# One more pair of gates taken plainly, a store moved to another queue, and operands split earlier at three stage ends

## The chip, the cores and the metric

The kernel runs on one core of one Trainium2 chip. The metric is the device time of one execution in microseconds (us). PE is the matrix engine (TensorE), DVE the vector engine, ACT the scalar engine, POOL is GpSimd, and SP is the queue from which most transfers are issued. POOL has a queue of its own for transfers.

## The reference

One transformer-like layer on a sequence of 1024 tokens of width 1024, in fp32. What matters here, cut down:

```python
h = rmsnorm(x, g_mix_pre) * (1.0 + scale_m) + shift_m
z = h @ w_in                      # q, k, v, forget, pool, conv columns, and 3 x 1024 gate columns gl
br_a = forgetting_attention(q, k, v, fl + b_f)       # 8 heads x 64
br_b = pool_mixer(pu, w_pool, pool_scale)            # 256 columns
br_c = short_conv(ch, cb, cc, conv_w)                # 256 columns
gates = sigmoid(gl).reshape(b, s, 3, d)
merged = gates[0]*(br_a @ wa) + gates[1]*(br_b @ wb) + gates[2]*(br_c @ wc)
x  = x + gate_m * rmsnorm(merged @ w_out, g_mix_post)
h2 = rmsnorm(x, g_ff_pre) * (1.0 + scale_f) + shift_f
return x + gate_f * rmsnorm(square(relu(h2 @ w_ff1)) @ w_ff2, g_ff_post)
```

## The kernel before, in words

Every fp32 operand of a matrix product is split into two parts that PE takes at full rate: a high part (ACT copies it, names ending in h or hi) and a low part (DVE subtracts the high part, names ending in l or lo). A product is then three matmuls: high by high, high by low, low by high. `split` (lines 113 to 115) and `fsplit` (686 to 688) are these two instructions. Nearly every matmul is 128x128 by 128x512.

The stages, one after the other on PE: normalisation and the v columns; the attention with its projections; the gates; the branches; the output projection with the second normalisation and the transposes of `h2` (`out_tile`, `h2T_pair`); the first feed-forward matrix (FFN1); the second (FFN2); the final norm. The order of the instructions on each engine is set when the program is built, by a scheduler that works from the order of the code and the dependences; each engine then runs its own list in that order, and each instruction waits for what it needs. So an instruction that waits also holds up what stands behind it on its engine or queue.

**Gates.** There are 24 blocks of 128 gate columns: 3 branches b by 8 column blocks j. `gate(j, b)` (line 607) takes one block plainly: `load_w`, then two halves of 24 matmuls each in a "mm" bank (`gemm_T`, line 343), each half followed by a sigmoid on ACT (line 610) and a store to DRAM on POOL's queue. Two blocks, (0, 1) and (1, 1), are taken so (lines 731, 732); their matmuls stand among those of the attention. The other 22 are taken two at a time by `gate_pair` (line 796), a Strassen-like scheme with 7 products of 12 matmuls, 84 instead of 96. It needs sums of halves of `h` (t1p, t2p, g, sn: lines 751 to 782) and of the weights: `o` is the split of the first weight block r1, `o21` that of a sum s21 with the second block r2 (`sums_21`), `o34` and `o4` come from `sums_34`. The loop over `todo` (line 857) runs 11 pairs; each pair from the second on also loads four tiles of w_ada, which DVE reduces (`more_ada`). `mod_rows` (line 665), behind the pair i == 9, transposes two small rows of gate vectors on PE and stores them to `gr_d` on the SP queue (line 677). The M pool has 8 slots of 4 KB a partition, taken in turn by weights, sums, branch operands and the two `gr` rows.

**Branches.** `to_branches` (line 850), called inside the last pair, splits the branch operands 4 to 7 (loaded by `load_br` ahead of the last pair); behind the loop the operands 0 to 3 are loaded, then three gates (`load_sig`), then the first block of w_branch (`load_wb`, line 908). The loop over j (line 920) takes 48 matmuls a step.

**FFN1.** Bank names are X, Y and Z. `first_two(j)` (line 1085) computes the first two products of pair j and `relu2` (DVE, line 1073) squares the rectified sum; five of these (`EARLY`) run ahead while ACT and DVE build the sums T1 to T4. `last_five(j)` does the rest; its last lines rectify bank X on ACT (1110) and square on DVE. `h2T_pair(3, ...)` transposes the last quarter of `h2` in between, in the two Z banks.

**FFN2.** `parts` (line 1194) splits one step's operands u and w on ACT and DVE, `step` (1184) issues its 24 matmuls.

## Time and profile before

| | |
|---|---|
| time, median of 3 runs (lowest, highest) | 1501.37 us (1499.16, 1501.98) |
| the profiled execution: its time, its span | 1502.08 us, 1500.2 us |
| mean granted clock of PE | 0.976 of 2.4 GHz |
| busy share: PE, DVE, ACT, POOL | 95%, 68%, 42%, 15% |
| data moved over the span | 209 MB, 139 GB/s |

All times in the views are us from the start of the span. The span is 1.9 us shorter than the execution's time. PE is busy for 1422.0 us of 1500.2: nearly all of the rest lies in the stage ends, and the views that show where are the waits of PE (summed by the line that waited and by what released it) and the timeline (each row: start, duration, engine, line, operation, written<-read tiles, shape, and in brackets the idle time ahead of it with what ended that). A matmul's duration is longer than its share of the pipeline; what one costs is the step from one start to the next.

### The profile page before, as it was taken

What the parts mean: (1) busy time and instruction counts of PE and PEld (TensorE: products, weight loads), DVE (VectorE), ACT (ScalarE), POOL (GpSimd) and SP (SyncE); (2) the same over time, 40 slices, a digit from 0 to 9 for tenths busy, and PEclk for the clock granted to TensorE, in tenths of its full rate; (3) what the DMA queues carried; (4) which work ended last, traced back from release to release, by engine and by line L of the source; (5) the groups of instructions that cost most, each with busy time, mean ns of one, the idle gap of its engine ahead of it and who ended that gap; (6) DMA issues with size and microseconds to landing.
All of it is one profiled execution on the core that took longest, in us unless ns stands there. A gap on an engine that the chain in (4) does not pass through costs nothing. (4 is left out here: it accounts for less than half of the span.)

```text
span 1500.2 us, 18468 instructions
## 1 busy us (share of the span) xinstructions
PE 1422.0 (95%) x6587; PEld 1161.2 (77%) x6587; DVE 1027.5 (68%) x1906; ACT 626.8 (42%) x1098; POOL 231.4 (15%) x329
## 2 busy tenths in 40 slices
PE   6999999999889999769999899999999999999997
PEld 5898888788768877548878677888888788888875
DVE  7653589787999764247756598555554346997587
ACT  4622466557664333231136553333332243344343
POOL 6301334333301111000002001111111000000230
PEclk9999999999899999879999999999999999999999
DMA  7511101201148653356624444333321596545333
GB/s 265 201 43 44 56 29 57 86 29 69 44 142 293 227 191 130 142 180 225 209 76 141 174 149 152 120 105 113 112 99 71 216 331 231 162 140 158 124 105 133
DMA packets 64821, 209.02 MB, mean 139 GB/s; under 512 B 8841, under 2 KB 9945, under 8 KB 64730
## 3 DMA queue, kind: packets, MB, share of 16 engines
q1 hardware_dynamic: 55002, 176.38, 34.9%
q0 software_dynamic: 9728, 31.47, 5.6%
q8 instruction: 52, 0.85, 0.2%
q14 instruction: 39, 0.32, 0.1%
HBM read 163.73 MB, written 44.09 MB: 139 GB/s over the span
## 5 line engine op out<-in xcount | busy, mean ns | idle before, releaser
L687 ACT ACTIVATE uh<-u 128x1024 fp32r<-128x1024 f32 x56 | 59.4, 1060 | 161.4 <-PE X L1191 71.6
L688 DVE TENSOR_TENSOR ul<-u,uh 128x1024 fp32r<-128x1024 f32 x56 | 69.3, 1237 | 79.0 <-ACT uh L687 79.0
L688 DVE TENSOR_TENSOR op<-s,op 128x1024 fp32r<-128x1024 f32 x54 | 65.9, 1222 | 62.3 <-ACT op L687 62.3
L1190 PE MATMUL X<-wh,uh 128*128 128x512 f32 x256 | 100.5, 395 | 2.6 <-ACT wh L687 2.6
L1191 PE MATMUL X<-wl,uh 128*128 128x512 f32 x256 | 101.2, 395 | 1.6 <-DVE wl L688 1.6
L1192 PE MATMUL X<-wh,ul 128*128 128x512 f32 x256 | 100.6, 393 | 0.0
L352 PE MATMUL ps_mm<-hT,whi 128*128 128x512 f32 x240 | 95.9, 399 | 0.0
L353 PE MATMUL ps_mm<-hT,whi 128*128 128x512 f32 x240 | 95.4, 398 | 0.0
L354 PE MATMUL ps_mm<-hT,wlo 128*128 128x512 f32 x240 | 95.4, 397 | 0.0
L1074 POOL DMA_DIRECT2D u_d<-ur x64 | 34.5, 540 | 317.4 <-DVE ur L1073 317.4
L232 DVE CUSTOM_DVE_ANT_0 wa<-wa,cb,colt 128x1024 f32<-128x1024 f32 x48 | 62.8, 1319 | 23.0 <-DMA wa<-in_w_ada_dram 22.9
L687 ACT ACTIVATE op<-s 128x1024 fp32r<-128x1024 f32 x54 | 56.9, 1055 | 45.7 <-PE Y L720 22.0
L1191 PE MATMUL Y<-wl,uh 128*128 128x512 f32 x192 | 75.1, 391 | 0.0
L1192 PE MATMUL Y<-wh,ul 128*128 128x512 f32 x192 | 74.7, 389 | 0.0
L1190 PE MATMUL Y<-wh,uh 128*128 128x512 f32 x192 | 72.1, 389 | 0.0
L688 DVE TENSOR_TENSOR wl<-w2r,wh 128x1024 fp32r<-128x1024 f32 x56 | 69.3, 1238 | 0.2 <-ACT wh L687 0.2
L543 PE MATMUL ps_av<-PT,vS 128*128 128x256 f32 x320 | 63.1, 304 | 6.1 <-DVE att L547 3.3
L516 POOL TENSOR_SCALAR prob<-prob,sm 128x128 f32<-128x128 f32 (+3 forms) x64 | 52.8, 826 | 90.7 <-DVE sm L515 84.1
L543 PEld LDWEIGHTS ps_av<-PT,vS 128*128 128x128 f32 x320 | 49.9, 195 | 20.1 <-ACT PT L114 11.0
L1300 POOL TENSOR_TENSOR yl<-sn,gfb 128x512 f32<-128x512 f32 x12 | 24.2, 2029 | 260.0 <-DVE ul L688 244.0
L687 ACT ACTIVATE wh<-w2r 128x1024 fp32r<-128x1024 f32 x56 | 58.7, 1049 | 5.7 <-DVE w2r L1275 1.8
L1191 PEld LDWEIGHTS X<-wl,uh 128*128 128x128 f32 x256 | 48.7, 190 | 13.8 <-DVE wl L688 3.7
(436 smaller groups left out, 4105.4 us busy)
## 6 DMA issues: line engine op xcount, KB each, us to landing
w2r<-in_w_ff_dram SPq DMA_DIRECT2D x64, 512.0 KB, 3.7
wa<-in_w_ada_dram SPq DMA_DIRECT2D x48, 512.0 KB, 5.0
w1r<-in_w_ff_dram SPq DMA_DIRECT2D x37, 512.0 KB, 4.0
u_d<-ur POOLq DMA_DIRECT2D x64, 256.0 KB, 2.3
u<-u_d SPq DMA_DIRECT2D x32, 512.0 KB, 4.7
sig_d<-sig POOLq DMA_DIRECT2D x48, 256.0 KB, 2.9
sig<-sig_d SPq DMA_DIRECT2D x48, 256.0 KB, 3.6
w1r<-in_w_in_dram SPq DMA_DIRECT2D x22, 512.0 KB, 4.5
```

Source lines behind the costliest of these rows:

```text
L232: V.tensor_tensor_reduce(out=w, in0=w, in1=cbs[0], scale=1.0, scalar=colt[:, C_BADA + i:C_BADA + i + 1], op0=ALU.mult, op1=ALU.add, accum_ ...
L352: T.matmul(p, a, r0, start=(i == 0), stop=False)
L353: T.matmul(p, a, r1, start=False, stop=False)
L354: T.matmul(p, b, r0, start=False, stop=(i == n - 1))
L516: G.tensor_scalar(pr_[:, :L], pr_[:, :L], sm, 0.0, op0=ALU.mult, op1=ALU.add)
L543: last_pe[0] = T.matmul(av[:, :256], st, PT[:, pp, offs[jj]:offs[jj] + 256], start=(j == 0 and pp == 0), stop=(j == nj - 1 and pp == 1))
L687: A.activation(hi, src, AF.Copy)
L688: V.tensor_tensor(out=lo, in0=src, in1=f32(hi), op=ALU.subtract)
L1074: nc.gpsimd.dma_start(u_d[q][j // 2][:, j % 2, :], r)
L1190: T.matmul(bank[t], a, r0, start=(first and k == 0), stop=False, skip_group_check=True)
L1191: T.matmul(bank[t], a, r1, start=False, stop=False, skip_group_check=True)
L1192: T.matmul(bank[t], b, r0, start=False, stop=(last and k == 1), skip_group_check=True)
```

## The change

Five edits:

1. The loop `for b in (1, 2): for j in (0, 1): gate(j, b)` takes four blocks plainly instead of two; `todo` starts two entries later, so 10 pairs remain.
2. Each pair's `r1` and `o` are made by a new function `gate_op` one pair ahead.
3. `mod_rows` is called behind pair i == 8, now the last but one, and its two stores go to POOL's queue.
4. The loads of the branch operands 4, 5, 6 and of the first block of w_branch stand inside the last pair, right behind its r2; `to_branches` splits 4 and 5, the block of w_branch, then 6; 7 and 0 to 3 follow. The M pool holds the block and its two parts.
5. FFN1 and FFN2: the transposes of the last quarter use banks Z, Z, X, X; in the first five `first_two` the rectifying and squaring is done by ACT (two instructions) instead of DVE (one); and the operands of FFN2's first two steps are written ahead of the last rectified sum of FFN1, with FFN1's banks closed behind it.

```diff
-            nc.sync.dma_start(gr_d[i:i + 1, :].rearrange("o (j p) -> (o j) p", p=P), gr)
+            nc.gpsimd.dma_start(gr_d[i:i + 1, :].rearrange("o (j p) -> (o j) p", p=P), gr)
...
-    gate(0, 1)
-    gate(1, 1)
+    for b in (1, 2):
+        for j in (0, 1):
+            gate(j, b)
...
+    def gate_op(b, j):
+        r1 = load_half(w_in[16 + 3 * j + b])
+        o = g_op()
+        fsplit(o[:, 0, :], o[:, 1, :], r1)
+        return r1, o
+    todo = [(b, j) for j in range(0, KT, 2) for b in (1, 2, 0)][2:]
+    nxt_op = gate_op(*todo[0])
...
-    def gate_pair(b, j, first, hook):
-        r1 = load_half(w_in[16 + 3 * j + b])
-        o = g_op()
-        fsplit(o[:, 0, :], o[:, 1, :], r1)
+    def gate_pair(b, j, r1, o, first, hook):
         r2 = load_half(w_in[16 + 3 * (j + 1) + b])
+        if hook:
+            for k in (4, 5):
+                load_br(k)
+            wb_0.append(load_half(w_branch[0]))
+            load_br(6)
         s21, o21 = sums_21(g_op, r1, r2)
...
-        for k in (4, 5, 6, 7):
+        for k in (4, 5):
             split_br(k)
+        hi, lo = (sb("M", F32R, name=n) for n in ("wbh", "wbl"))
+        split(hi, lo, wb_0[0])
+        wb_0[:] = [hi, lo]
+        split_br(6)
+        load_br(7)
-    todo = [(b, j) for j in range(0, KT, 2) for b in (1, 2, 0)][1:]
...
-        if last:
-            for k in (4, 5, 6, 7):
-                load_br(k)
-        gate_pair(b, j, i == 0, to_branches if last else None)
+        gate_pair(b, j, *nxt_op, i == 0, to_branches if last else None)
+        if not last:
+            nxt_op = gate_op(*todo[i + 1])
         if i:
             more_ada(4)
-        if i == 9:
+        if i == 8:
             mod_rows()
...
+    split_br(7)
     for k in (0, 1, 2, 3):
         load_br(k)
...
-    wts = load_wb(0)
+    wts = wb_0
...
-        relu2(0, j, plus(Y, s1))
+        c = plus(Y, s1)
+        if j < EARLY:
+            r = tile_of(fpool, "ur", 3, (P, HALF))
+            A.activation(c, c, AF.Relu)
+            A.activation(r, c, AF.Square)
+            nc.gpsimd.dma_start(u_d[0][j // 2][:, j % 2, :], r)
+        else:
+            relu2(0, j, c)
...
+        if j == NJ - 1:
+            return X
         c = tile_of(fpool, "sn", 3, (P, HALF))
         A.activation(c, X, AF.Relu)
         relu2(1, j, c)
...
-    h2T_pair(3, pairs[3], lambda: fbank("Z", 2), lambda: tile_of(fpool, "ur", 3, (P, HALF)))
+    z_x = ["Z", "Z", "X", "X"]
+    z_n = {"Z": 2, "X": 5}
+    def t_bank():
+        tag = z_x.pop(0)
+        return fbank(tag, z_n[tag])
+    h2T_pair(3, pairs[3], t_bank, lambda: tile_of(fpool, "ur", 3, (P, HALF)))
...
-    for n in ("fpool", "tpool", "mpool", "h2pool", "fps"):
+    for n in ("fpool", "tpool", "mpool", "h2pool"):
         close_pool(n)
     gpool = open_pool("gpool")
-    gps = open_pool("gps", space=bass.MemoryType.PSUM)
...
-    X = banks("X")
-    for kk in range(NK):
-        if kk < 2:
-            pace[0] = None
+    def first_parts(kk):
         uA.append(load_u(0, kk, "uA", NK))
         b11 = load_b(0, kk)
         if kk >= 2:
             uB.append(load_u(1, kk - 2, "uB", NK))
-        step(X, kk, *parts(uA[kk], b11), first=kk == 0, last=kk == NK - 1)
+        return parts(uA[kk], b11)
+    early = []
+    for kk in range(2):
+        pace[0] = None
+        early.append(first_parts(kk))
+    c, r = (g2("sn", 12, shape=(P, HALF)) for _ in range(2))
+    A.activation(c, X_last, AF.Relu)
+    V.scalar_tensor_tensor(out=r, in0=c, scalar=0.0, in1=c, op0=ALU.max, op1=ALU.mult)
+    nc.gpsimd.dma_start(u_d[1][(NJ - 1) // 2][:, (NJ - 1) % 2, :], r)
+    close_pool("fps")
+    gps = open_pool("gps", space=bass.MemoryType.PSUM)
+    X = banks("X")
+    for kk in range(NK):
+        step(X, kk, *(early[kk] if kk < 2 else first_parts(kk)), first=kk == 0, last=kk == NK - 1)
```

What this does to the built order, at three places.

ACT's list from the end of the attention into the first pair of gates, before; `op` is the high part of the first weight block, the following `op` that of the first sum s21, `g` are high parts of the sums of `h`:

```order
L546 ACTIVATE avt<-ps_av_4297 64x256
L687 ACTIVATE g_605_4458<-t2p_4475 128x512
L687 ACTIVATE g_601_4454<-t1p_4474 128x512
...
L687 ACTIVATE g_604_4457<-t1p_4494 128x512
L687 ACTIVATE op_4473<-w1r_4514 128x1024
L687 ACTIVATE op_4523<-s_627_4520 128x1024
```

The same place in the changed program; `sig` are the sigmoids of the plain gates, each of which reads a bank that 24 matmuls have filled:

```order
L546 ACTIVATE avt<-ps_av_4297 64x256
L610 ACTIVATE sig_4509<-ps_mm_4484 128x512
L610 ACTIVATE sig_4543<-ps_mm_4518 128x512
L610 ACTIVATE sig_4571<-ps_mm_4546 128x512
L687 ACTIVATE op_4597<-w1r_4598 128x1024
L687 ACTIVATE g_619_4582<-t2p_4603 128x512
...
L687 ACTIVATE g_618_4581<-t1p_4622 128x512
L687 ACTIVATE op_4647<-s_641_4644 128x1024
```

Three sigmoids, those of the last 72 plain matmuls, now stand ahead of the first pair's `op`, and the eight `g` behind it. On PE, 24 of the 96 added plain matmuls stand among the last instructions of the attention, and 72 behind the last of them, ahead of the first pair.

DVE's list at the last pair of gates, before (DMAHW in the brackets is the landing of a transfer of the SP queue, DMASW of one of POOL's; `s_853` is the last pair's s21):

```order
L676 COPY gr_5967<-ps_pu_5965 8x128 [waits PE_49]
L688 TENSOR_TENSOR op_5980<-w1r_5978,op_5980 128x1024 [waits DMAHW2_49,Activation_49]
L697 TENSOR_TENSOR s_853_5985<-w1r_5983 128x512 [waits DMAHW5_49,DMAHW3_49,DVE_49]
L705 TENSOR_TENSOR s_860_6037<-w1r_5978,w1r_5983 128x512 [waits DMAHW6_49,DVE_49]
L698 TENSOR_TENSOR s_853_5985<-s_853_5985,w1r_5978 128x512 [waits DVE_49]
```

The same place in the changed program, where `s_849` is s21, `s_856` is s34, and `wbl_6106` the low part of the first block of w_branch:

```order
L676 COPY gr_5966<-ps_pu_5964 8x128 [waits PE_49]
L688 TENSOR_TENSOR oc_6037<-w1r_5969,oc_6037 128x512 [waits DMAHW5_49,DVE_49,Activation_49]
L726 TENSOR_TENSOR sn_5998<-ps_av_6000,sn_5998 128x512 [waits DVE_49,PE_49]
L697 TENSOR_TENSOR s_849_5979<-w1r_5969 128x512 [waits DMASW3_49,DVE_49]
L705 TENSOR_TENSOR s_856_6031<-w1r_5930,w1r_5969 128x512 [waits DMASW5_49,DVE_49]
L698 TENSOR_TENSOR s_849_5979<-s_849_5979,w1r_5930 128x512 [waits DVE_49]
L706 TENSOR_TENSOR s_856_6031<-w1r_5930,s_849_5979 128x512 [waits DVE_49]
L115 TENSOR_TENSOR wbl_6106<-w1r_5975,wbh_6105 128x1024 [waits DMAHW0_49,DVE_49,Activation_49]
L688 TENSOR_TENSOR op_5982<-s_849_5979,op_5982 128x1024 [waits Activation_49]
```

The low part of `o` is gone from here (made a pair earlier); s21 now stands behind `sn_5998`, the sum that needs the pair's second product, and waits for the landing of a `gr` store (DMASW3), whose slot of the M pool it takes; `wbl_6106` stands ahead of the low part of o21 (`op_5982`). On SP the two loads of the last pair (line 692) no longer stand behind the `gr` stores.

ACT's list at the change from FFN1 to FFN2, before (`sn` is the last rectified bank of FFN1):

```order
L1078 ACTIVATE sn_10023<-Z_10010 128x512
L1110 ACTIVATE sn_10069<-X_9947 128x512
L687 ACTIVATE uh_10093<-u_10089 128x1024
L687 ACTIVATE wh_10097<-w2r_10091 128x1024
L687 ACTIVATE uh_10129<-u_10125 128x1024
```

And in the changed program:

```order
L1096 ACTIVATE sn_10022<-Z_10009 128x512
L1267 ACTIVATE sn_10099<-X_9946 128x512
L687 ACTIVATE uh_10079<-u_10075 128x1024
L687 ACTIVATE wh_10083<-w2r_10077 128x1024
L687 ACTIVATE uh_10091<-u_10087 128x1024
```

The code now writes uh and wh ahead of this `sn`; in the built list they still stand behind it.

## Rows read from the trace of the kernel before

**Rows 1.** Waits of PE over the whole span: us in total, times, longest us

```profile
PE ps_mm L718 <- ACT op L687: 16.1, 2, 10.5
...
PE ps_s L352 <- ACT wbh L114: 13.8, 1, 13.8
...
PE X L1190 <- ACT wh L687: 2.6, 1, 2.6
```

**Rows 2.** Timeline of PE at the first pair: start, us, instruction, [idle before]

```profile
418.69 0.79 PE L718 MATMUL ps_mm<-hT,op 128*128 128x512 f32 x1 [5.58 <-ACT op L687]
...
421.65 0.63 PE L720 MATMUL ps_mm<-hT,op 128*128 128x512 f32 x1
...
423.52 0.39 PE L719 MATMUL ps_av<-hT,op 128*128 128x512 f32 x1
...
423.75 0.39 PE L720 MATMUL ps_av<-hT,op 128*128 128x512 f32 x1
```

**Rows 3.** Timeline of ACT, end of the attention and first pair

```profile
397.67 1.28 ACT L610 ACT_TABLE_LOAD   x1
...
398.97 0.60 ACT L610 ACTIVATE sig<-ps_mm 128x512 f32<-128x512 f32 x1
...
399.58 1.28 ACT L514 ACT_TABLE_LOAD   x1
...
417.59 1.05 ACT L687 ACTIVATE op<-w1r 128x1024 fp32r<-128x1024 f32 x1
```

**Rows 4.** Waits of the SP queue between 600 and 700 us

```profile
SPq L677 <- DVE gr L676: 39.0, 1, 39.0
```

**Rows 5.** Timeline of the SP queue, last pair and branches

```profile
619.67 0.67 SPq L677 DMA_DIRECT2D gr_d<-gr  x2
...
621.80 1.13 SPq L692 DMA_DIRECT2D w1r<-in_w_in_dram  x2
...
652.96 4.71 SPq L901 DMA_DIRECT2D sig<-sig_d  x6
...
657.78 10.34 SPq L910 DMA_DIRECT2D raw<-in_w_branch_dram  x4
```

**Rows 6.** Timeline of ACT, last pair and branches

```profile
628.81 1.06 ACT L687 ACTIVATE op<-w1r 128x1024 fp32r<-128x1024 f32 x1 [8.91 <-DMA w1r<-in_w_in_dram]
...
664.19 1.06 ACT L114 ACTIVATE wbh<-raw 128x1024 fp32r<-128x1024 f32 x1 [6.91 <-DMA raw<-in_w_branch_dram]
```

**Rows 7.** Transfers (page, part 6): queue, count, KB each, us to landing

```profile
sig_d<-sig POOLq DMA_DIRECT2D x48, 256.0 KB, 2.9
```

**Rows 8.** Timeline of PE, from the gates into the branches

```profile
651.08 0.39 PE L720 MATMUL ps_mm<-g,oc 128*128 128x512 f32 x1
...
665.30 0.79 PE L352 MATMUL ps_s<-brh,wbh 128*128 128x512 f32 x1 [13.84 <-ACT wbh L114]
...
679.56 0.39 PE L352 MATMUL ps_s<-brh,wbh 128*128 128x512 f32 x1
...
690.76 0.39 PE L352 MATMUL ps_s<-brh,wbh 128*128 128x512 f32 x1
```

**Rows 9.** Timeline of DVE, same place

```profile
651.16 8.14 DVE L115 TENSOR_TENSOR brl<-brr,brh 128x1024 fp32r<-128x1024 f32 x7 [0.57 <-ACT brh L114]
```

**Rows 10.** Timeline of PE in FFN1

```profile
907.96 0.80 PE L718 MATMUL X<-t,op 128*128 128x512 f32 x1 [3.10 <-ACT op L687]
...
913.67 0.40 PE L720 MATMUL X<-t,op 128*128 128x512 f32 x1
```

**Rows 11.** Timeline of DVE, same place

```profile
903.11 1.29 DVE L1073 SCALAR_TENSOR_TENSOR ur<-sn 128x512 f32<-128x512 f32 x2
```

**Rows 12.** Windows: us, busy (x) of PE, PEld, DVE, ACT, POOL, clock, DMA share, GB/s

```profile
402.00:411.00 9.00, 7.65 (x30) 6.49 (x30) 6.96 (x12) 3.00 (x7) 2.32 (x3) 0.50 0.01 2
...
870.00:908.00 38.00, 34.88 (x149) 27.05 (x147) 37.72 (x64) 17.74 (x30) 3.77 (x7) 0.98 0.35 125
```

**Rows 13.** Timeline of ACT at the start of FFN2

```profile
1177.91 0.60 ACT L1110 ACTIVATE sn<-X 128x512 f32<-128x512 f32 x1 [7.65 <-PE X L720]
```

More of the change, by code (lines that the diff above doesn't have):

```diff
@@ L839 @@
     brr = {}
+    wb_0 = []
     def load_br(k):
@@ L1153 @@
         else:
-            last_five(j, *first_two(j))
-    for n in ("fpool", "tpool", "mpool", "h2pool", "fps"):
+            X_last = last_five(j, *first_two(j))
+    for n in ("fpool", "tpool", "mpool", "h2pool"):
         close_pool(n)
     gpool = open_pool("gpool")
-    gps = open_pool("gps", space=bass.MemoryType.PSUM)
     NK = NJ // 2
```

## The prediction

> **What bounds the kernel now.** PE is busy 95% of the span, so a change pays where it removes matmuls, where it removes idle time of PE, or where it spares PE the lower clock that follows idle time. I read the summed waits of PE first: two lines of the gates (16.1 us in two waits, and 13.8 in one) are more than any others of the whole span, and the change touches both [rows 1]. The timeline at each then shows what ended the wait, and what the clock did: behind the first pair's wait of 5.58 us, six steps from one matmul to the next take 2.96 us (418.69 to 421.65), and later a step takes 0.23 us (423.52 to 423.75), so the slow start costs 2.96 - 6 x 0.23 = 1.6 us more [rows 2]. 0.49 against 0.23 a step, partly waits, fits the two clock levels, 1.2 and 2.4 GHz. I use 1.6 us for a restart after idle time where no row of its own stands here. The profiled execution took 1502.1 us, the median of the runs is 1501.4; the sum is made against the first and taken off the second, 0.7 us lower.
>
> **Edit 1, four plain blocks instead of two.** A pair goes: 84 matmuls, 84 x 0.23 = 19.3 us. 96 plain ones come. By the built order 24 of them stand among the last matmuls of the attention, where PE ran at the lower clock throughout, 0.50, and was idle in between (7.65 us busy of 9), so it waited for ACT and DVE there [rows 12]; I count these 24 at nothing, and if that cover fails they cost 24 x 0.23 = 5.5. The other 72 cost 72 x 0.23 = 16.6. The balance is -2.7.
>
> The wait of 5.58 us in front of the first pair [rows 2] should become shorter, since DVE can make the sums of `h` beside the 72 matmuls. It will not vanish. ACT's `op` (417.59, 1.05 us) ended it [rows 3], and in the new order it stands behind the last sigmoid (0.60), which needs the last plain matmul: 1.65 us idle at least. Then the low part of `op`, 1.16 (8.14 us for seven of that size [rows 9]), and eight `g` on ACT at about 0.5 each ahead of the next high part, while PE has 24 matmuls, 5.5 us, in hand. I take 6 us lost instead of 5.6 + 1.6 = 7.2, a gain of 1.2. Edit 1: **-4**; between +3 (the 24 cost 5.5, the stall stays) and -10 (the stall goes).
>
> Each sigmoid between exponentials also cost ACT two table loads of 1.28 us [rows 3]. The built lists hold seven loads from the attention on to the first pair instead of nine, for the new sigmoids stand together. That is 2.6 us of ACT, which I count at nothing on PE's path, being inside the cover above. The Trainium skill, "ScalarE: Activation LUTs", section "What ACT_TABLE_LOAD costs", prices a switch at about 2.66 us with a drain of 1.38 behind the load. Here the sigmoid starts 1.30 us after its load does, so the trace shows no such drain; by the page the two loads would be worth 5.3 us of ACT instead of 2.6, and if all of that were on the path the sum would be 5.3 lower.
>
> **Edit 2, `o` one pair ahead.** Within the steady pairs PE waits little; the 0.23 us step is already PE's own. Nothing, except at the last pair.
>
> **Edit 3, the last pair.** Here PE was idle 10.5 us [rows 1], with 1.6 for the restart 12.1. The chain: SP's queue waited 39.0 us at the store of `gr` for DVE's copy [rows 4]; the two loads of the last pair stood behind it and were issued at 621.80 [rows 5]; ACT waited 8.91 us for them and began `op` at 628.81 [rows 6]. In the new order neither load is behind those stores, and `o` is already there. So the first two products, 24 matmuls or 5.5 us, run at once. Late next is o21. Its sum s21 stands on DVE behind the sum that reads the second product (0.6 at 5.5 us), then four operations of 0.6 (1.29 - 0.69 [rows 11]), of which three are needed: 7.9. ACT's high part, 1.05: 9.0. DVE's low part, behind the fourth sum and the new `wbl`: 8.5 + 1.16 + 1.16 = 10.8. PE idles from 5.5 to 9.0, does two matmuls, waits about 1.4 for the low part: 4.9, and 1.2 to 1.6 for the clock: 6.3. The new wait for the landing of the `gr` store hides in this: about 1 us for the copy and the issue, and 2.9 to the landing by the nearest row, which is of a much bigger store on POOL's queue [rows 7], make 3.9, ahead of 6.1. Edit 3: 12.1 - 6.3 = **-6**; between 0 (the store or `wbh` comes so late that the stall is as before) and -9 (DVE in time).
>
> **Edit 4, into the branches.** The gates' last matmul starts at 651.08 and ends its step at 651.3 (E). Step j=1 of the branches starts at 679.56, E + 28.2; a step takes 690.76 - 679.56 = 11.2 [rows 8]. So 17.0 us were lost: the wait of 13.84, and 48 matmuls at a clock that rose late. The wait was for w_branch's first block, issued at 657.78 behind six loads of gates (652.96 [rows 5]) and ready for ACT at 664.19 [rows 6]. In the new order this block is loaded and split beside the last pair. The operands come next: before, DVE's seven last low parts ran from 651.16 to 659.3, E - 0.1 to E + 8.0 [rows 9]. The new order has them in the sequence in which PE needs them, 4 and 5 first, and PE takes 24 matmuls, 5.6 us, with 4 to 7, so from 1.16 a part PE starts within 1 us of E and ends j=0 at about E + 12. Then it is j=1 that needs a block of w_branch that still stands behind the gate loads: by the old row at most 664.19, E + 12.9, with 1.05 for ACT E + 13.9, with DVE's part 1.2 later, and PE does eight matmuls that need the high part alone first. I take j=1 at the full step from E + 16, clock included, against E + 28.2: **-12**. Ends: -5 (operands late at j=0 as well, 8 us, and 4 at j=1) and -15.5 (one restart remains).
>
> **Edit 5.** In FFN1 PE waited 3.10 us at 907.96, then took 5.71 us for 13 steps, to 913.67, instead of 3.0 [rows 10]: 5.8 lost. DVE was busy 37.72 of the 38 us before, ACT 17.74 [rows 12]. Five squares go from DVE, 5 x 0.6 = 3.0 [rows 11]; ten instructions of some 0.5 come to ACT, which has 20 us free. The wait then shrinks to about nothing, and with it the slow steps; but DVE, still full, used those slow steps to catch up, and part comes back as short waits: **-4**; between 0 and -5.8. The new banks for the transposes move nothing on PE, where they did not wait before: 0.
>
> At FFN2 PE waited 2.6 us [rows 1], and the restart cost as much again. ACT rectified the last bank at 1177.91 [rows 13], then split u and w. In the built list that order is unchanged, whatever the code says: **0**.
>
> Sum: -4 - 6 - 12 - 4 = **-26**, 1476.1 for the profiled execution, **1475.4** for the median.
>
> **The rivals.**
> (A) The branches are bound by their operands: eight low parts with the new `wbl` among them, and loads that before had 14 us of PE's idle time to run ahead. For it: DVE takes 8.1 us for seven parts in a row [rows 9]. Against it: the parts come in PE's order. Edit 4 then gives 5, and the time is 1482.5.
> (B) The `gr` stores land late and the last pair stalls as before, at s21 instead of `op`: edit 3 gives 0, 1481.5. It decides if a landing takes over 2.4 us more than the 2.9 of the row. Against it: 4 KB instead of 256 [rows 7]. The Trainium skill, "DMA: Bandwidth & Descriptors", section "Issuing engine by pattern", gives plain stores to SP's queue as the generally faster one; no row here has both queues with one size.
> (C) The early split at FFN2 works after all, because the list is not what decides: 2.6 and as much again come off, 1470.
> (D) Slower: the clock stays at 1.2 GHz through the added plain matmuls, because the attention's tail leaves PE idle between them, as it was at 0.50 for 9 us [rows 12]. Then all 96 cost about 0.43 instead of 0.23 and none is hidden: 41 us against 19.3 saved, +22; the stall at the first pair stays. It makes the whole slower if the other edits then give less than 22, as with A and B (4 + 5 = 9): 1514. It decides from the point where the 72, which stand in one run with nothing between, do not bring the clock back; the first pair's own run did so [rows 2], hence the small chance.
> (E) The edits move waits only and nothing is gained: 1501. Against it stand three stalls whose causes by name are gone from the lists.
>
> **How the numbers follow.** The forecast has 0.55, A 0.18, B 0.12, C 0.08, D 0.04, E 0.03. A measurement of this kernel tells about 0.2%, 3 us. Faster by more than that: the first four, 0.93; same 0.03; slower 0.04. The range takes in A, B and C, and the bounds of the terms as far as they are likely together: **1463 to 1490**, the upper end being A with B and a bit more, the lower end the forecast with the first pair's stall gone and the best of edit 4 and edit 5.
>
> **What would show each step.** Edit 1: a wait of about 2 us in front of the first pair. Edit 3: no wait at the last pair's first matmul, one of 3 to 4 us at its third product, released by ACT's `op`. Edit 4: j=0 starting within 2 us of the gates' end, and a short wait at j=1 on `wbh`. Edit 5: the wait at 907.96 under 1.5 us; the one into FFN2 still about 2.6. I am wrong if a first pair, last pair or j=0 waits 8 us or more, or if the branches from j=1 on take more than 11.6 us a step.

## The result, and the profile after

The changed kernel takes 1475.8 us (median of four runs, 1473.9 to 1478.5); the kernel before took 1500.6 us in the runs beside it (1499.2 to 1502.0). The ratio is 0.9836, 95% interval 0.9816 to 0.9856: 24.9 us faster. The prediction was 1475.4, its likeliest case. The profiled execution took 1473.9 us, span 1472.1, the fastest of the four, so the stages below add up to 28.1 us and not 24.9; PE is busy 1416.8 us of it (before 1422.0), at a mean clock of 0.990 (before 0.976).

Five points that both programs pass and the end, read from the timeline of PE (us from the start of the span), give the ledger:

| point | before | after | won up to here | won in the stage | the sum had |
|---|---|---|---|---|---|
| transposes of the rows, last pair begins | 619.05 | 612.80 | 6.25 | 6.25 (edits 1, 2) | 4 |
| last matmul of the gates | 651.08 | 639.54 | 11.54 | 5.29 (edits 2, 3) | 6 |
| branches, step j=2 | 690.76 | 668.19 | 22.57 | 11.03 (edit 4) | 12 |
| FFN1, first product | 860.17 | 837.60 | 22.57 | 0.00 | 0 |
| FFN2, first matmul | 1180.44 | 1151.30 | 29.14 | 6.57 (edit 5) | 4 |
| end of the span | 1500.2 | 1472.1 | 28.1 | -1.04 | 0 |

The summed waits of PE, where [rows 1] had 16.1, 13.8 and 2.6:

```profile
PE ps_mm L718 <- ACT op L687: 5.7, 2, 4.1
...
PE ps_s L352 <- ACT wbh L114: 4.2, 1, 4.2
...
PE X L1224 <- ACT wh L687: 2.6, 1, 2.6
```

The gates keep 5.7 us in two waits, the branches 4.2; the wait at FFN2 is what it was. The wait at FFN1, 3.10 us in [rows 10], is gone from the list.

**First pair** (timeline of PE: start, us, instruction, idle ahead):

```profile
409.14 1.00 PE L543 MATMUL ps_av<-PT,vS 128*128 128x256 f32 x7
...
409.98 0.39 PE L352 MATMUL ps_mm<-hT,whi 128*128 128x512 f32 x1
...
426.48 0.40 PE L354 MATMUL ps_mm<-hT,wlo 128*128 128x512 f32 x1
...
428.50 0.50 PE L718 MATMUL ps_mm<-hT,op 128*128 128x512 f32 x1 [1.63 <-ACT op L687]
428.84 0.39 PE L719 MATMUL ps_mm<-hT,op 128*128 128x512 f32 x1
429.07 0.40 PE L718 MATMUL ps_av<-hT,op 128*128 128x512 f32 x1
429.76 0.50 PE L720 MATMUL ps_mm<-hT,op 128*128 128x512 f32 x1 [0.29 <-DVE op L688]
```

The attention's last matmuls start at 409.14. 72 plain matmuls follow from 409.98 on without a gap; the wait behind them is 1.63 us, against 5.58 in [rows 2], and no slow matmuls follow it: from the second matmul to the third a step takes 0.23 us (428.84 to 429.07). The windows that answer to [rows 12] (columns as there):

```profile
402.00:411.00 9.00, 9.00 (x58) 7.59 (x57) 8.85 (x16) 3.92 (x8) 2.71 (x4) 1.00 0.08 29
...
847.00:885.00 38.00, 38.00 (x167) 30.98 (x166) 37.37 (x62) 24.64 (x44) 4.32 (x8) 1.00 0.37 129
```

From 402 to 411 us PE is busy all the time at 1.00, before it was 7.65 us busy at 0.50. In FFN1 PE has no gap in 38 us, with DVE as full as before and ACT at 24.64 us instead of 17.74. The two stretches of 38 us stand some 23 us apart, as the program does.

**Last pair**, PE, then DVE:

```profile
612.94 0.48 PE L718 MATMUL ps_mm<-hT,op 128*128 128x512 f32 x1
...
618.37 0.40 PE L720 MATMUL ps_av<-hT,op 128*128 128x512 f32 x1
...
622.83 0.79 PE L718 MATMUL ps_mm<-g,op 128*128 128x512 f32 x1 [4.07 <-ACT op L687]
...
624.53 0.80 PE L720 MATMUL ps_mm<-g,op 128*128 128x512 f32 x1
...
628.96 0.44 PE L719 MATMUL ps_s<-g,op 128*128 128x512 f32 x1
```

```profile
618.80 0.69 DVE L726 TENSOR_TENSOR sn<-ps_av,sn 128x512 f32<-128x512 f32 x1 [0.95 <-PE ps_av L720]
...
619.41 0.68 DVE L697 TENSOR_TENSOR s<-w1r 128x512 f32<-128x512 f32 x1
...
620.61 0.69 DVE L698 TENSOR_TENSOR s<-s,w1r 128x512 f32<-128x512 f32 x1
...
622.11 1.23 DVE L115 TENSOR_TENSOR wbl<-w1r,wbh 128x1024 fp32r<-128x1024 f32 x1
...
623.25 2.35 DVE L688 TENSOR_TENSOR op<-s,op 128x1024 fp32r<-128x1024 f32 x2
```

The first product begins at 612.94 without a wait, the third waits 4.07 us. DVE's sum that reads the second product stands at 618.80, s21 follows at once (619.41, 620.61). On ACT:

```profile
620.77 1.06 ACT L114 ACTIVATE wbh<-w1r 128x1024 fp32r<-128x1024 f32 x1 [0.57 <-DVE s L705]
...
621.74 1.99 ACT L687 ACTIVATE op<-s 128x1024 fp32r<-128x1024 f32 x2
...
654.22 1.06 ACT L114 ACTIVATE wbh<-raw 128x1024 fp32r<-128x1024 f32 x1 [7.24 <-DMA raw<-in_w_branch_dram]
```

The split of w_branch's first block (620.77) stands ahead of that of s21 (621.74), which ends the wait. From 622.83 the matmuls run at 0.43 us a step until 628.96.

**Branches**, PE, then SP's queue:

```profile
639.54 0.40 PE L720 MATMUL ps_mm<-g,oc 128*128 128x512 f32 x1
...
639.77 0.39 PE L352 MATMUL ps_s<-brh,wbh 128*128 128x512 f32 x1
...
655.33 0.50 PE L352 MATMUL ps_s<-brh,wbh 128*128 128x512 f32 x1 [4.21 <-ACT wbh L114]
...
668.19 0.39 PE L352 MATMUL ps_s<-brh,wbh 128*128 128x512 f32 x1
```

```profile
645.78 2.69 SPq L919 DMA_DIRECT2D sig<-sig_d  x6
...
648.58 0.36 SPq L928 DMA_DIRECT2D raw<-in_w_branch_dram  x1
```

The step j=0 follows the gates without a gap (639.77). j=1 waits 4.21 us: w_branch's second block was issued at 648.58, behind six gate loads (645.78), and reached ACT at 654.22. At FFN2 the row that answers to [rows 1] and [rows 13] is

```profile
1151.30 1.22 PE L1224 MATMUL X<-wh,uh 128*128 128x512 f32 x2 [2.58 <-ACT wh L687]
```

### The profile page after: what moved, and what is told of

The parts are those of the page before. It is cut to its first block, busy times and chain, and to the rows that moved or that the text cites. A ratio compares the mean times of both kernels' runs of the same rounds, so it can differ in the third digit from the quotient of the medians.

```text
span 1472.1 us, 18484 instructions
## 1 busy us (share of the span) xinstructions
PE 1416.8 (96%) x6599; PEld 1158.3 (79%) x6599; DVE 1018.6 (69%) x1892; ACT 624.3 (42%) x1100; POOL 232.4 (16%) x332
## 5 line engine op out<-in xcount | busy, mean ns | idle before, releaser
L352 PE MATMUL ps_mm<-hT,whi 128*128 128x512 f32 x272 | 108.5, 399 | 0.0
L354 PE MATMUL ps_mm<-hT,wlo 128*128 128x512 f32 x272 | 108.3, 398 | 0.0
L353 PE MATMUL ps_mm<-hT,whi 128*128 128x512 f32 x272 | 108.0, 397 | 0.0
L1092 POOL DMA_DIRECT2D u_d<-ur x58 | 31.3, 540 | 245.9 <-DVE ur L1091 245.9
L543 PE MATMUL ps_av<-PT,vS 128*128 128x256 f32 x320 | 60.0, 294 | 2.4 <-ACT PT L114 1.3
```

Of the source, the lines that this page charges most:

```text
L352: T.matmul(p, a, r0, start=(i == 0), stop=False)
L353: T.matmul(p, a, r1, start=False, stop=False)
L354: T.matmul(p, b, r0, start=False, stop=(i == n - 1))
L543: last_pe[0] = T.matmul(av[:, :256], st, PT[:, pp, offs[jj]:offs[jj] + 256], start=(j == 0 and pp == 0), stop=(j == nj - 1 and pp == 1))
L1092: nc.gpsimd.dma_start(u_d[q][j // 2][:, j % 2, :], r)
```

## The experiments

All times are medians; a difference from the changed kernel is worked out from the two ratios to the kernel before, times 1500. Each ratio has an interval of about 0.002 on either side, 3 us, so differences of less than some 4 us are read from the stages of the profiles, where the rest of the program is the same. Each program has one profile, and a stage scatters too: the last pair takes 26.15 to 26.74 us in the seven programs that leave its order alone, and the time from FFN2's first matmul to the end is 318.8 to 320.8 us in the eleven changed programs that do not touch it.

**Edit 1 taken back.**

```diff
-    for b in (1, 2):
+    for b in (1,):
         for j in (0, 1):
             gate(j, b)
...
-    todo = [(b, j) for j in range(0, KT, 2) for b in (1, 2, 0)][2:]
+    todo = [(b, j) for j in range(0, KT, 2) for b in (1, 2, 0)][1:]
...
-        if i == 8:
+        if i == 9:
             mod_rows()
```

> The changed kernel with edit 1 taken back: two plain blocks, 11 pairs, the row stores behind the last pair but one as before; all other edits stay. Theory: the 6.2 us that the changed kernel has won by the last pair's transposes (612.80 against 619.05) come from edit 1, so this kernel takes about 1482 us, 6 more than the 1475.8 of the changed one, with 0.50 as granted clock between 402 and 411 us and a wait of 4 to 6 us in front of the first pair. Rival: they come from edit 2 (the next pair's first split made one pair ahead); then the time stays within 2 us of 1475.8 and only the place of the stall changes.

1480.9 us, ratio 0.9868 (0.9849 to 0.9888): 4.8 us slower than the changed kernel. The transposes come at 622.64, 9.8 later than in the changed kernel; from the gates' end to j=2 it is 3.1 us shorter (25.5 against 28.65), which gives part of that back. In front of the first pair PE waits only 1.42 us, not 4 to 6: with `o` made ahead, the pair starts early and waits later, 2.2 and 1.7 us in front of its next products. The clock between 402 and 411 is 0.81, where 0.50 was expected. So the gain is edit 1's (with edit 1 and without edit 2, in the last run but one below, the transposes come at 612.59); the place of the remaining waits was expected wrongly.

**The 24 matmuls out of the attention's tail.**

```diff
+        if b == 2:
+            wts = load_w(w_in[16 + 3 * j + b], split)
+            for hf in range(2):
+                with tc.issue_after(last_pe[0].ins):
+                    pp = gemm_T(wts, hT, K8, hf, "mm")
+                ev(pp, hf, slice(hf * HALF, (hf + 1) * HALF))
+            return
         proj(16 + 3 * j + b, ev)
```

> The changed kernel, but all matmuls of the two added plain blocks are ordered behind the attention's last matmul; before, 24 of them stood among its last matmuls. Theory: the 24 do more than hide (24 x 0.23 = 5.5 us): they keep PE's clock at 2.4 GHz in the attention's tail and so let it end 3 us earlier (410.0 against 413.1). Then the window 402 to 411 us shows 0.50 again, the attention ends near 413, and the time is 8 to 9 us above 1475.8, about 1484. Rival, as in the prediction's term: the 24 are only hidden, and the time is 5.5 us above, about 1481.

1485.0 us, ratio 0.9894 (0.9869 to 0.9919): 8.7 us slower. That is the value of the theory, but with some 5 us on either side it does not exclude the rival's 5.5; the profile has to tell them apart. The window 402 to 411 us and the tail of PE's timeline:

```profile
402.00:411.00 9.00, 6.01 (x31) 5.10 (x31) 7.79 (x14) 5.09 (x11) 2.29 (x3) 0.81 0.05 19
```

```profile
403.79 0.35 PE L543 MATMUL ps_av<-PT,vS 128*128 128x256 f32 x1 [3.32 <-DVE att L547]
...
412.51 0.39 PE L352 MATMUL ps_mm<-hT,whi 128*128 128x512 f32 x1
...
436.62 0.50 PE L725 MATMUL ps_mm<-hT,op 128*128 128x512 f32 x1 [1.63 <-ACT op L694]
```

The wait of 3.3 us is back and the clock falls (0.81 over the window; 0.50 was expected). The first pair starts at 436.62 instead of 428.50, 8.1 us: the run of plain matmuls begins 2.5 us later (412.51 against 409.98), behind a tail that ends later, and is 5.6 longer by its 24 matmuls. The attention's first products began at 156.89 and 156.80, so the shift is not older. The wait in front of the first pair is the same 1.63 us.

**The row stores back on SP's queue.**

```diff
-            nc.gpsimd.dma_start(gr_d[i:i + 1, :].rearrange("o (j p) -> (o j) p", p=P), gr)
+            nc.sync.dma_start(gr_d[i:i + 1, :].rearrange("o (j p) -> (o j) p", p=P), gr)
```

> The changed kernel with the two row stores back on SP's queue; they still stand behind the last pair's two weight loads there, with the branch operands and w_branch's first block behind them. Theory: what took the 10.5 us stall away is that the last pair's loads and first split no longer stand behind the stores, not POOL's queue as such; the block of w_branch is loaded a little later, and the time is within 2 us of 1475.8. Rival: with SP held up again the block of w_branch comes late, ACT's split of it stands ahead of o21, and the last pair's stall of 4.1 us becomes 8 or more: about 1481.

1476.6 us, ratio 0.9840 (0.9816 to 0.9864): no difference (0.6 us). The last pair's third product waits 4.38 us instead of 4.07: ACT waits 0.89 us for w_branch's block, so the rival's chain is there, but small. With edit 2 in place POOL's queue as such brings nothing.

**Edit 4 taken back.**

```diff
-        if hook:
-            for k in (4, 5):
-                load_br(k)
-            wb_0.append(load_half(w_branch[0]))
-            load_br(6)
...
+        if last:
+            for k in (4, 5, 6, 7):
+                load_br(k)
         gate_pair(b, j, *nxt_op, i == 0, to_branches if last else None)
...
-    wts = wb_0
+    wts = load_wb(0)
```

> The changed kernel with edit 4 taken back: w_branch's first block is loaded and split behind the gate loads, and the branch operands 4 to 7 are loaded ahead of the last pair, as before. Theory: edit 4 is worth 11.0 us (the step j=2 starts 22.6 us earlier than before, the gates end 11.5 us earlier), so the time is about 1487, with one wait of 13 to 14 us in front of j=0 instead of 4.2 in front of j=1. Rival: a part of it came from the earlier loads that edits 1 to 3 allow; then the wait is 8 us or less and the time about 1481.

1483.4 us, ratio 0.9888 (0.9867 to 0.9907): 7.8 us slower. On PE:

```profile
622.04 0.79 PE L718 MATMUL ps_mm<-g,op 128*128 128x512 f32 x1 [3.73 <-ACT op L687]
...
651.89 0.79 PE L352 MATMUL ps_s<-brh,wbh 128*128 128x512 f32 x1 [13.50 <-ACT wbh L114]
```

The wait in front of j=0 is 13.5 us, as before. From the gates' end to j=2 it takes 39.25 us, against 28.65 in the changed kernel and 39.68 before: 10.6 for edit 4. The last pair is 1.1 us shorter (0.5 against the shortest of the others); in ACT's list w_branch's split no longer stands ahead of s21's. The theory holds for the stage; the time was expected at 1487.

**The squares back on DVE.**

```diff
-        c = plus(Y, s1)
-        if j < EARLY:
-            r = tile_of(fpool, "ur", 3, (P, HALF))
-            A.activation(c, c, AF.Relu)
-            A.activation(r, c, AF.Square)
-            nc.gpsimd.dma_start(u_d[0][j // 2][:, j % 2, :], r)
-        else:
-            relu2(0, j, c)
+        relu2(0, j, plus(Y, s1))
```

> The changed kernel with the first five squares of FFN1 back on DVE (one instruction instead of two on ACT). Theory: FFN1 is 6.6 us shorter in the changed kernel because DVE, busy without a break there, is relieved of 5 x 0.6 = 3.0 us, which takes away a wait of 3.1 us and the restart at the lower clock (2.7 us): the wait returns and the time is about 1481.5 to 1482. Rival: the banks X for the transposes gave it; then the time stays within 1.5 us of 1475.8.

1483.8 us, ratio 0.9885 (0.9869 to 0.9902): 7.4 us slower. The wait returns to the hundredth of a us, against [rows 10]:

```profile
885.89 0.79 PE L718 MATMUL X<-t,op 128*128 128x512 f32 x1 [3.10 <-ACT op L687]
```

FFN1 takes 320.70 us from its first product to FFN2's first matmul, 320.27 before, 313.70 in the changed kernel. The squares carry all of it.

**The banks and FFN2's operands taken back.** The edit undoes the lines on `z_x`, `t_bank`, `X_last` and `early`.

> The changed kernel with the two other parts of edit 5 taken back: all four transposes of the last quarter in the Z banks, and FFN2's first operands written behind the last rectified sum. Theory: both are worth nothing, since PE did not wait at the transposes and the built list splits the operands behind the rectifying either way: within 1.5 us of 1475.8, with the wait of 2.58 us in front of FFN2 unchanged. Rival: the banks carry 1 to 3 us of FFN1's 6.6: 1477 to 1479.

1475.0 us, ratio 0.9826 (0.9805 to 0.9847): no difference. FFN1 takes 313.36 us, and the wait at FFN2 is 2.58.

**The rows in tiles of their own.**

```diff
-            gr = sb("M", shape=(8, P), name="gr")
+            gr = (small.tile([P, P], F32, tag="nckd", name="gr", bufs=1) if i else
+                  const.tile([P, P], F32, name="gr", tag="wpb", bufs=1))[:8, :]
```

> The changed kernel with the two small rows in tiles that are out of use by then instead of two slots of the M pool. Theory: in the changed kernel s21 of the last pair stands on DVE behind the pair's second product because its slot was taken by such a row; with the slot free the built list has s21 and its split one pair earlier, the wait of 4.07 us and the slow matmuls behind it (2.8 us) go, and the time is about 1469.5. Rival: the split of w_branch's first block, which now stands ahead of o21 on ACT and DVE, is what is late, and it moves along: then the wait stays at 3 us or more.

1467.1 us, ratio 0.9774 (0.9760 to 0.9789): 9.3 us faster than the changed kernel. In the last pair (columns as in [rows 12]):

```profile
614.00:633.00 19.00, 19.00 (x85) 15.46 (x84) 4.34 (x8) 6.12 (x10) 2.90 (x7) 1.00 0.33 115
```

PE has no gap and the full clock. From the transposes to the gates' end it takes 19.29 us instead of 26.74, 7.5 won. On DVE the last pair's s21 now stands a pair earlier, ahead of the transposes at 614.25:

```profile
594.76 0.69 DVE L698 TENSOR_TENSOR s<-w1r 128x512 f32<-128x512 f32 x1
```

w_branch's split also moved up and was not in the way. j=1 still waits, 4.59 us.

**w_branch's second block ahead of the gate loads.**

```diff
+    raw1 = b_raw()
+    nc.sync.dma_start(raw1, w_branch[1])
     for i in range(3):
         load_sig(i)
...
-        raw = b_raw()
-        nc.sync.dma_start(raw, w_branch[j])
+        raw = raw1 if j == 1 else b_raw()
+        if j > 1:
+            nc.sync.dma_start(raw, w_branch[j])
```

> The changed kernel with the load of w_branch's second block ahead of the first six loads of gates on SP's queue instead of behind them. Theory: the 4.21 us in front of j=1 are the wait for this load (ACT waited 7.24 us for it), and with it some 2.2 us of slow matmuls go: about 1469.5. Rival: the loads of gates, now later, hold up the eviction of j=0's banks on DVE, and j=1 waits for DVE instead: a gain of 3 us or less.

1470.7 us, ratio 0.9794 (0.9777 to 0.9811): 6.3 us faster. On PE:

```profile
651.31 0.40 PE L352 MATMUL ps_s<-brh,wbh 128*128 128x512 f32 x1
...
663.71 0.50 PE L352 MATMUL ps_s<-brh,wbh 128*128 128x512 f32 x1 [1.10 <-ACT wbh L114]
```

j=1 starts without a wait; j=2 now has one of 1.10 us. The stage takes 23.98 us instead of 28.65, 4.7 won. j=1 did not wait for DVE, so the rival is out.

**Three together**, with FFN2's first step split ahead of the last rectified sum (the diff shows this third part):

```diff
-    A.activation(c, X_last, AF.Relu)
+    with tc.issue_after(last_wl[0].ins):
+        A.activation(c, X_last, AF.Relu)
```

> The changed kernel with three things together: the two small rows in tiles of their own, w_branch's second block loaded ahead of the gate loads (both ran alone before this), and at the start of FFN2 the last rectified sum of FFN1 ordered behind the split of the first step's operands, on ACT and so on DVE. Theory: the first two add up, about 8.5 and 5 us by their own runs, and the third takes away the wait of 2.58 us at FFN2 and as much again for the restart at the lower clock, 5 us: 1475.8 - 18.5, about 1457. Rival: the third does nothing, because the first matmul then waits for u or w to land or for DVE's low part, and the time is about 1462.

1460.1 us, ratio 0.9739 (0.9723 to 0.9756): 14.6 us faster than the changed kernel. FFN2's first matmul:

```profile
1139.27 0.49 PE L1230 MATMUL X<-wh,uh 128*128 128x512 f32 x1 [0.69 <-ACT sn L1275]
```

The wait is 0.69 us instead of 2.58, and what ends it is ACT's rectifying itself. From FFN1's first product to the end it takes 630.1 us instead of 634.5. The other programs without this part, the one with the squares on DVE left out, take 632.6 to 634.1 there, so the third part is worth 2.5 to 4.4 of the 5 expected. The others: 19.29 us for the last pair, and 24.2 from the gates' end to j=2, as each had it alone. The sum is 3 us short, about the width of the interval.

**Four together: the last plain sigmoids behind the first pair's split.**

```diff
+            if (b, j) != (2, 1):
+                gate(j, b)
+    wts = load_w(w_in[16 + 3 * 1 + 2], split)
+    late = [gemm_T(wts, hT, K8, hf, "mm") for hf in range(2)]
     close_pool("big")
...
+    for hf in range(2):
+        sig_out(2, 1, hf, late[hf])
```

> As e9_three, and the sigmoids of the last plain block are written behind the first pair's first split, so that ACT's list has this split and the eight high parts of the sums of h ahead of them. Theory: the wait of 1.63 us in front of the first pair is ACT's sigmoid (0.60) and split (1.05) behind the last plain matmul; with the split ahead of them it goes, and the smaller waits of the pair shrink: 2 to 3 us under e9_three. Rival: the first pair then waits just as long for DVE's low parts or for a bank: within 1 us of e9_three.

1453.7 us (five runs, 1452.2 to 1456.6), ratio 0.9693 (0.9678 to 0.9707): the fastest version, 21 us under the changed kernel and 46 under the one before. PE at the first pair:

```profile
428.30 0.39 PE L354 MATMUL ps_mm<-hT,wlo 128*128 128x512 f32 x1
...
428.53 0.39 PE L721 MATMUL ps_mm<-hT,op 128*128 128x512 f32 x1
```

There is no wait any more, and from here to the third pair's first matmul it takes 41.22 us instead of 43.85: with the wait 4.3 us won in this place. The profiles of this and the run before differ by only 2.5 us in span; the profiled execution, the slowest of this version's five, had lost 1.4 ahead of the attention's products. The medians differ by 6.4, of which 4.3 are placed.

**Edit 2 taken back.**

```diff
-    nxt_op = gate_op(*todo[0])
...
-        gate_pair(b, j, *nxt_op, i == 0, to_branches if last else None)
-        if not last:
-            nxt_op = gate_op(*todo[i + 1])
+        gate_pair(b, j, *gate_op(b, j), i == 0, to_branches if last else None)
```

> The changed kernel with edit 2 taken back: each pair's first split is made in the pair itself; the row stores stay on POOL's queue. Theory: what freed the last pair is that its loads no longer stand behind the row stores on SP's queue; either of POOL's queue and edit 2 does that, so the last pair's wait at its first matmul is about 2 us (ACT's split), not 10.5, and s21, which then stands ahead of the second product's sum on DVE, costs less than 4 us; the first pair waits about 3 to 4 us longer, since its split stands behind the eight g. Time within 4 us of 1475.8. Rival: edit 2 alone took the stall away; then the last pair waits 8 us or more and the time is above 1482.

1471.4 us, ratio 0.9813 (0.9798 to 0.9828): 3.5 us faster than the changed kernel. The first pair and the last pair:

```profile
432.58 0.79 PE L718 MATMUL ps_mm<-hT,op 128*128 128x512 f32 x1 [5.78 <-ACT op L687]
...
614.43 0.50 PE L718 MATMUL ps_mm<-hT,op 128*128 128x512 f32 x1 [1.46 <-ACT op L687]
```

The first pair waits 4.2 us longer (5.78), the last one 1.46 us at its first matmul and not at all at the third product (23.83 us from the transposes to the end, instead of 26.74: 2.9 won). But the late start of the first pair is made up within two pairs. The third pair's first matmul, in this run and in the changed kernel:

```profile
472.74 0.40 PE L718 MATMUL ps_mm<-hT,op 128*128 128x512 f32 x1
...
472.40 0.40 PE L718 MATMUL ps_mm<-hT,op 128*128 128x512 f32 x1
```

With edit 2 PE starts the first pair early and then waits six more times in the first two pairs, 3.5 us in all, for low parts on DVE and sums on ACT; here it waits in front only. In the ten programs that have edit 2 and the same pairs the first two take 41.2 to 44.6 us from the first matmul on, in the two without it 40.2 and 41.0. From the third pair to the transposes there is no difference: 139.2 to 142.6 us in the ten, 139.9 and 140.2 in the two. So edit 2 wins nothing before the last pair, and in the last pair it costs 2.9 us.

**Edit 2 taken back and the row stores on SP's queue.** As above, with the line of the third experiment.

> As e11_op_not_ahead, and the row stores back on SP's queue, where the built list has them ahead of the last pair's second weight block and behind its first. Theory: now SP's queue is held up again, ACT gets the second block and w_branch's first some 5 us after the rows' copy, and the last pair's third product waits 5 us or more longer than in e11_op_not_ahead: 3 to 7 us slower than that. Rival: the queue costs nothing here either (within 2 us of e11_op_not_ahead), as with edit 2 in place.

1474.9 us, ratio 0.9838 (0.9822 to 0.9854): 3.8 us slower than with POOL's queue. On PE:

```profile
617.38 0.50 PE L718 MATMUL ps_mm<-hT,op 128*128 128x512 f32 x1 [1.46 <-ACT op L687]
...
627.23 0.80 PE L718 MATMUL ps_mm<-g,op 128*128 128x512 f32 x1 [3.20 <-ACT op L687]
```

The third product waits 3.20 us where it did not wait in the run before (5 or more were expected), and the last pair takes 26.69 us instead of 23.83. The chain on ACT:

```profile
625.17 1.06 ACT L114 ACTIVATE wbh<-w1r 128x1024 fp32r<-128x1024 f32 x1 [3.27 <-DMA w1r<-in_w_branch_dram]
626.13 1.99 ACT L687 ACTIVATE op<-s 128x1024 fp32r<-128x1024 f32 x2
```

w_branch's first block, issued at 618.30 behind the stores, comes late, and ACT's split of it stands ahead of that of s21. Here the queue counts, 2.9 us in this place.

## Why the prediction was right, and where its steps were off

**Edit 1** had -4, and the ledger shows 6.25 for edits 1 and 2 together; by the run without edit 2 it is all edit 1's. It adds up from four terms. The pair that went gives 18.6 (from the third pair to the transposes 140.40 us instead of 158.99; 19.3 in the sum), the 72 plain matmuls cost 16.9 (16.6), and the first two pairs, with the wait in front of them, take 7.0 us more than 2 x 19.29 instead of 8.4, 1.4 won (1.2). These three came near what was worked out. The step that was mis-sized is the one on the 24 matmuls in the tail ("I count these 24 at nothing"): the attention ends 3.1 us sooner, and 2.5 of that go when they are moved out (second experiment). Without them the tail has its wait of 3.3 us and a clock of 0.81, with them no wait and 1.00. How much of the 2.5 is the clock and how much the changed order no run separates. The wait in front of the first pair was put at 1.65 us at least, from ACT's sigmoid and split behind the last plain matmul; it is 1.63, and the run with four parts took it away by changing that order alone. Rival (D) is out: the 72 run at 0.23 us a step.

**Edit 2** was "nothing, except at the last pair". For the pairs ahead of the last one this holds: by the third pair's first matmul its early start is worth 0.34 us (472.40 and 472.74), and from there to the last pair nothing that stands clear of the scatter. At the last pair the sum counted on it, since `o` is already there; it does take away a wait of 1.46 us there, but with it s21 stands on DVE behind the second product, and without it ahead. On balance edit 2 costs 2.9 us in that place with the rows on POOL's queue, and nothing with them on SP's (26.67 and 26.69 us for the last pair).

**Edit 3** had 12.1 - 6.3 = 6, and 5.3 came. The 6.3 were 4.9 of waits and 1.2 to 1.6 of clock; measured are 4.07, and about 2.8 for 14 steps at 0.43. The order in time was right to a few tenths (s21 begun at 6.5 us from the pair's start, 6.1 in the sum; its high part begun at 8.8, 7.9 in the sum). What lay behind that order was priced only in part: that s21 takes the slot of a row was on record ahead of the result, but the sum took the slot for a wait for the store's landing, which "hides in this". As a wait at run time it does, the stores land in 1.6 and 1.9 us; but because of that slot the built list has s21 behind the second product, and the rows in tiles of their own are worth 7.5 us in the stage, 9.3 by the medians. As for the cause of the old stall, the row of 39.0 us on SP's queue was read rightly, but no single edit took it away: with the stores back on SP, with the branch loads back, or without edit 2, the last pair waits 3.7 to 4.4 us, or 1.5, never 10.5. With two of the three taken back it waits 1.46 and 3.20 us, and the last pair takes 2.9 us longer than with edit 2 alone taken back. Taking back all three was not tried, so which of them together took the 10.5 us away stays open.

Rival (B), with the stores landing late, is out: 1.6 and 1.9 us against the 2.9 of [rows 7]. The Trainium skill, "DMA: Bandwidth & Descriptors", section "Issuing engine by pattern", gives plain stores to SP as the generally faster queue. Here the third experiment shows no loss from POOL's, and without edit 2 the time is 3.8 us longer with SP's, for what stands behind the stores.

**Edit 4** had -12; 11.0 came, 10.6 by the undo. j=0 starts at the gates' end, as worked out. The wait at j=1 was put at some 2 us (j=0 done at E + 12, the high part at E + 13.9), and is 4.21, since the block reached ACT at E + 14.5 instead of E + 12.9 (E is 639.77). That this load stands behind the gate loads was read rightly; moving it ahead is worth 4.7 us in the stage. Behind its wait j=1 itself takes 12.9 us; from j=2 on a step takes 11.2. Rival (A) is out.

**Edit 5** had -4, "part comes back as short waits"; nothing came back, PE has no gap, and the stage is 6.6 us shorter. The cause, five squares of 0.6 us on a DVE without a break, is shown by the undo. Of the 6.6, 5.8 are the wait and the restart; the other 0.8 we have not placed. At FFN2 the forecast of nothing is right to the hundredth, 2.58 and 2.58, so rival (C) is out; the early split, worth 5 by the sum, came out at 2.5 to 4.4 once the order was really changed.

**Table loads.** They went from nine to seven up to the first pair, as the lists said. Three lines before, two after:

```profile
L610 ACT ACT_TABLE_LOAD x4 | 5.1, 1283 | 0.1
L514 ACT ACT_TABLE_LOAD x4 | 5.1, 1283 | 0.1
...
L789 ACT ACT_TABLE_LOAD x1 | 1.3, 1283 | 0.0
```

```profile
L610 ACT ACT_TABLE_LOAD x4 | 5.1, 1283 | 0.1
...
L514 ACT ACT_TABLE_LOAD x3 | 3.8, 1283 | 0.1
```

Two loads, 2.6 us of ACT, are gone; what that was worth to PE no run tells. The drain of 1.38 us that the Trainium skill states ("ScalarE: Activation LUTs", section "What ACT_TABLE_LOAD costs") shows in no row here: behind these loads the next activation starts 1.29 to 1.30 us after the load's start.

The total fits better than the terms: edit 1 and the squares were taken 4.8 us too low in the profiled executions, edits 3 and 4 1.7 too high, 1.0 was lost behind FFN2's start, and the profiled execution was 1.9 us faster than the median. That the median came within 0.4 us of the forecast is in part luck.

## What to carry to other kernels

Read the built order before you price an edit: here it told that one edit could do nothing and where three waits would come to stand, and the trace gave their sizes. A stall behind a queue that three edits touch need not come back when one of them is undone, and here not with two; no cause is named until the stall has been brought back. An early start is not a gain until the next point that both programs pass shows it: 4.2 us at the first pair were 0.3 two pairs later. Where an in-order list puts work later than its data allow, look for the buffer slot it takes; a tile of half a KB a partition decided 7.5 us of a stage.

## What was not expected of the hardware

- Matmuls that fill the gaps of a stage are worth more than their own time: with 24 in the attention's tail PE's clock stays at 1.00 over 402 to 411 us (without them 0.50 in the profile before and 0.81 in two others), and the attention itself ends 2.5 us sooner.
- A wait of 1.63 us in front of the first pair was followed by matmuls at the full step; one of 4.07 us in the last pair by 14 at 0.43 us. The length of the wait alone does not tell: with edit 1 taken back a wait of 1.42 us was followed by seven steps of about 0.43 us, behind a tail in which PE had been busy for 6.28 of the 9 us from 402 to 411.
- A store of 4 KB from POOL's queue landed in 1.6 and 1.9 us, one of 256 KB in a median of 2.9 in the profile before and 3.5 in the one after.
- One program's executions differ: the four of the changed kernel lie 4.7 us apart (1473.9 to 1478.5). Stages differ between programs that leave them alone as well: from the third pair to the last, 139.2 to 142.6 us in ten programs with edit 2. How much of this is the chip and how much small differences in the built order is not known; a difference of 3 us in one profile of this kernel is not yet a finding.
